# The first feed-forward's first pass: inner tiles that take 5 to 14 channel tiles, and another mix and pace behind it

## The chip, the core and the metric

The kernel runs on one core of one Trainium2 chip. TensorE (PE) multiplies, VectorE (DVE) and ScalarE (ACT) do the elementwise work, SyncE (SP) issues every DMA, GpSimd (POOL) does next to nothing. The metric is the time of one execution in device microseconds. Three runs of the kernel before gave a median of 1883.54 us (1883.38 to 1883.9).

## The reference, cut to what matters

One layer on 256 tokens of 2048 channels, in float32. The vector `c` gives nine modulation vectors of 2048 numbers each, by one matrix of 2048 x 18432.

```python
mod = silu(c) @ w_ada + b_ada                    # 2048 -> 9 x 2048
sh1, sc1, gt1, sh2, sc2, gt2, sh3, sc3, gt3 = split(mod, 9)
f = swiglu(modulate(rms_norm(h, g_ffn1), sh1, sc1), w1_gate, w1_up, w1_down)
h = h + 0.5 * gt1 * f
nrm = modulate(rms_norm(h, g_mix), sh2, sc2)
q, k, v = split(nrm @ w_qkv, 3)                  # then two kinds of attention
h = h + gt2 * mix
f = swiglu(modulate(rms_norm(h, g_ffn2), sh3, sc3), w2_gate, w2_up, w2_down)
h = h + 0.5 * gt3 * f
# swiglu(x) = (silu(x @ w_gate) * (x @ w_up)) @ w_down, inner width 5632
```

## The kernel before, in words

Channels lie in 16 tiles of 128 (`KT`), the inner width in 44 tiles (`FT`). All weights come in one stream (`W`, in the order of `srcs`) of chunks of 512 KB; a chunk is eight blocks of 128 x 128. A chunk in `rw` is split: ACT casts it to the short format (`hiw`, `wsplit`), DVE subtracts that from the original (`low`), and four buffers hold each (`LOB`). SP fetches three chunks ahead (`AHEAD`). The activations `nx[k]` are split in the same way.

A block costs PE a fixed amount. In the wide form (`mm2`) it is one matmul of 512 columns and one of 256; in the slim form (`mm3`) three of 256. The very first blocks are not split: there PE multiplies in float32 ("native", the loop over `K1` in `build`, line 561).

The modulation vectors are made beside it. One step takes a row block of `w_ada` (1 MB, `ada_issue`), and DVE reduces it against `cb` into one column of one vector (`ada_use`, tiles `ra` and `rx`, line 151). A channel tile `k` of `nx` needs two of them, the scale and the shift. Steps wait in the list `bg`. `bg_step` issues the DMA of the next step and, when all three buffers are taken, first reduces an older one; `pend` holds what is issued and not reduced yet. How many steps are made is set by `ws.pace(rate)`: each chunk fetched adds `rate` to a credit, and each whole credit makes one step. `bg_until(n)` makes steps until only `n` are left, and its reductions stand in the program where it is called.

The first feed-forward then runs in these passes.

- Native: inner tiles 0 to 7 take the first `K1` channel tiles while the modulation comes in.
- First part (`up_first`, tiles `pa`, weights `w1_a`): inner tiles 8 to 31 take the first `K1` channel tiles, too, at pace `RA`; even ones slim, odd ones wide. Each partial sum is parked in SBUF (`park`, `park2`, tiles `pt`).
- Later pass (`ffn`, tiles `pb`, weights `w1_b`): inner tiles 0 to 3 take the other channel tiles by the steps of `CUTS`, as they come; then 4 to 31 take theirs, each added to what was parked and passed through the gate on DVE and ACT (`up_finish`). The pace is `RB[0]`.
- Down (`ffn_down`, tiles `pd`, weights `w1_d`) at `RB[1]`; the twelve inner tiles left over, up (`pb`, `w1_c`) at `RB[2]` and down (`pd`, `w1_e`) at `RB[3]`. The last four are slim on the last output tile, `d` = 15.

From the last cut on, the list `bg` holds the 64 steps of the modulation vectors 2, 4, 3 and 5 (gate of this feed-forward; scale, shift and gate of the attention). After the last down pass `build` calls `bg_until(0)`, issues some idle matmuls (`idle(14)`, tile `pw`), and computes from the sum of squares (`stat`, `rstd_first`) the first `nx` of the attention, whose q, k and v matmuls (`pqv`, `pqk`, `pqq`) follow.

The order on each engine is a strict queue, made when the program is built: the framework sorts the instructions by program order, priority and its own estimate of when they are ready. PE alone keeps the order written in the attention.

Of the kernel before, what the change touches and what calls it, by code (L numbers as in the profile page):

```python
# [15 lines left out]
P = 128  # L16
S = 256
D = 2048
KT = D // P
DFF = 5632  # L20
FT = DFF // P
# [2 lines left out]
EPS = 1e-6  # L24
NEG = -1e30
CW = 1024
K1 = 6
K2 = 8
CUTS = (6, 8, 10, 12, 14, 16)
CUTS2 = (8, 12, 16)  # L30
NF0 = 8
NF1 = 4
NL = 4
ND = 3
F1 = 32
PLAN = ((4, 6, 9, 11), (8, 10, 13, 15), (12, 14, 17, 19), (16, 18, 21, 23))
PLAN_L = ((4, 6, 9, 11), (6, 8, 11, 13), (7, 9, 12, 14), (9, 11, 14, 15))
QS = 1
PACT = 0
RA = 0.455  # L40
RB = (0.28, 0.36, 0.36, 0.3)
RQ = 0.2
RE = 0.28
RF = (0.2, 0.2, 0.1, 0.1)
# [8 lines left out]
PLACE = ((44, 40),) + 7 * ((48, 0),)  # L53
KA = 3
SLIM = 4
MANUAL = {mybir.EngineType.PE}


# [10 lines left out]
def build(tc, a):  # L69
    nc = tc.nc  # L70
    with ExitStack() as ctx:
# [202 lines left out]
        def bg_add(ids, then=None):  # L274

            ids = list(ids)
            bg.extend((i, then if i == ids[-1] else None) for i in ids)
# [115 lines left out]
        ws = W()  # L393

        def up_first(f, part, kx, slim=False):
            ps = pair("pa")
            if slim:
                for j in range(2):
                    for k in range(kx):
                        wh, wl = ws.next()  # L400
                        mm3(ps[:, j, :S], wh, wl, nx[k][:, 0, :], nx[k][:, 1, :], k == 0, k == kx - 1)
                park(ps[:, :, :S], f, part)
                return
            up_mm(ps, 0, kx, True, True)
            park2(ps, f, part)
# [20 lines left out]
        def up_mm(ps, k0, k1, first, last):  # L426
            for j in range(2):
                for k in range(k0, k1):
                    mm2(ps[:, j, :], *ws.next(), nx[k], first and k == k0, last and k == k1 - 1)
# [17 lines left out]
        def ffn_down(fs, hid, gate, stat=None, out=None):  # L447
            acc_ = {}
            for d, f in down_order(fs):
                if d not in acc_:  # L450
                    acc_[d] = bank("pd")
                slim = d == KT - 1 and (stat is not None or out is not None)
                if slim:
                    wh, wl = ws.next()
                    mm3(acc_[d][:, :S], wh, wl, hid[f][:, 0, :], hid[f][:, 1, :], f == fs[0], f == fs[-1])
                else:
                    mm2(acc_[d], *ws.next(), hid[f], f == fs[0], f == fs[-1])
                if f != fs[-1]:
                    continue
                ps = acc_[d]  # L460
                g = gate(d)
                if d == KT - 1 and stat is not None:
                    idle(3)
                with tc.high_priority(offset=URGENT if stat is not None and d >= KT - 2 else 0):
                    for part_ in (ps[:, :S],) if slim else (ps[:, :S], ps[:, S:]):
                        nc.vector.scalar_tensor_tensor(h[d], part_, g, h[d], ALU.mult, ALU.add)  # L466
                    if stat is not None:
                        stat.add(h[d])
                        if d == KT - 1:
                            ws.split_late(stat.sq)  # L470
                if out is not None:
                    nc.sync.dma_start(out[d], h[d])

        def ffn(cuts, part, ready_k, gate, rates, stat=None, out=None):

            kx = cuts[0]
            hid = {}
            head = [pair("pb") for f in range(NF1)]
            for k0, k1 in zip(cuts, cuts[1:]):
                ready_k(k1)  # L480
                if k1 == KT:
                    late[:] = [True]
                    ws.pace(rates[0])
                for f in range(NF1):
                    up_mm(head[f], k0, k1, k0 == kx, k1 == KT)
                    if k1 == KT:
                        up_finish(f, head[f], part, hid)
            for f in range(NF1, F1):
                ps = pair("pb")
                up_mm(ps, kx, KT, True, True)  # L490
                up_finish(f, ps, part, hid)
            psum_pool("bank")
            ws.pace(rates[1])
            ffn_down(range(F1), hid, gate)
            psum_pool("pair")
            ws.pace(rates[2])
            for f in range(F1, FT):
                ps = pair("pb")
                up_mm(ps, 0, KT, True, True)
                up_finish(f, ps, {}, hid)  # L500
            ln_exp_set()
            psum_pool("bank")
            ws.pace(rates[3])
            ffn_down(range(F1, FT), hid, gate, stat, out)

# [4 lines left out]
        part = {}  # L510
# [41 lines left out]
        for k in range(K1):  # L552
# [4 lines left out]
            for j in range(2):  # L557
                w = ws.whole()
                for b in range(8):
                    f, q = 4 * j + b // 2, b % 2  # L560
# [8 lines left out]
                after(ins, casts[f // 3 - 1], "cast")  # L569
        psum_pool("pair")  # L570

        ws.pace(RA)
        for f in range(NF0, F1):
            up_first(f, part, K1, f % 2 == 0)
        st = Stat(KT)

        def rest1(k):
            bg_until(min(len(bg) + len(pend), (KT - k) * 2))
            if k < KT:
                return  # L580
            for j in (2, 4, 3, 5):
                bg_add(j * KT + k for k in range(KT))

        def once(l, fn):
            def get(d):
                if (l, d) not in gates:
                    gates[l, d] = fn(d)
                return gates[l, d]
            return get
# [4 lines left out]
            bg_until(min(len(bg) + len(pend), 4 * KT - d - 1))  # L594
            return mods[2][:, d : d + 1]

        ffn(CUTS, part, rest1, once(1, gate1), RB, stat=st)
        ws.pace(0.0)
        bg_until(0)
        idle(14)  # L600
# [289 lines left out]
            bg_until(min(len(bg) + len(pend), KT - d - 1))  # L890
            return mods[8][:, d : d + 1]

        ffn(CUTS2, part, rest2, once(3, gate3), RF, out=a["out"])
        psum_pool(None)
        ax_close()

# [1 line left out]
def _consts():  # L898
# [22 lines left out]

_SHAPES = {
    "x": (4, P, 4, S), "w_ada": (9 * KT, P, D), "vecs": (P, 224),
    "w1_s": (K1 * 2, P, CW), "w1_a": ((F1 - NF0) * 2 * K1 // 8, P, CW),
    "w1_b": (F1 * 2 * (KT - K1) // 8, P, CW), "w1_c": ((FT - F1) * 2 * KT // 8, P, CW),
    "w1_d": (KT * F1 // 8, P, CW), "w1_e": (KT * (FT - F1) // 8, P, CW),
    "w2_a": (F1 * 2 * K2 // 8, P, CW),
    "w2_b": (F1 * 2 * (KT - K2) // 8, P, CW), "w2_c": ((FT - F1) * 2 * KT // 8, P, CW),
# [6 lines left out]
def _arrays(inputs):  # L935
    g = {k: np.asarray(v) for k, v in inputs.items()}
    rope, lnc, nam, idx = _consts()
    c = np.ascontiguousarray

    def vec(v):  # L940
        return np.asarray(v).reshape(-1, P).T

    arr = {
        "x": c(g["x"][0].T.reshape(4, 4, P, S).transpose(0, 2, 1, 3)),
        "w_ada": c(g["w_ada"][0].reshape(D, 9 * KT, P).transpose(1, 2, 0)),
        "vecs": c(np.concatenate([
            vec(g["g_ffn1"][0]), vec(g["g_mix"][0]), vec(g["g_ffn2"][0]),
            vec(g["g_out_na"][0]), vec(g["g_out_dil"][0]), vec(g["c"][0]), vec(g["b_ada"][0])], axis=1)),
        "qkg": c(np.stack([g["qn_na"][0], g["kn_na"][0], g["qn_dil"][0], g["kn_dil"][0]])),
        "rope": rope, "lnc": lnc, "nam": nam,  # L950
        "nab": c(g["rpb_na"][0].reshape(8, -1)[:, idx].reshape(8, 2, P, S).transpose(0, 2, 1, 3)),
        "w_qkv": c(g["w_qkv"][0].reshape(8, 2, P, 3, 4, 512).transpose(4, 3, 0, 2, 1, 5)[:, ::-1].reshape(96, P, CW)),
        "w_o": c(g["w_o"][0].reshape(2, 8, P, KT, P).transpose(0, 3, 2, 1, 4).reshape(2 * KT, P, CW)),
    }

    def stream(blocks):
        return c(blocks.reshape(-1, 8, P, P).transpose(0, 2, 1, 3).reshape(-1, P, CW))

    for l in (1, 2):
        gu = np.stack([g[f"w{l}_gate"][0], g[f"w{l}_up"][0]]).reshape(2, KT, P, FT, P)  # L960
        gu = gu.transpose(3, 0, 1, 2, 4)
        cuts = CUTS if l == 1 else CUTS2
        kx = cuts[0]
        down = g[f"w{l}_down"][0].reshape(FT, P, KT, P).transpose(2, 0, 1, 3)

        def flat(x):
            return x.reshape(-1, P, P)

        if l == 1:
            arr["w1_a"] = stream(gu[NF0:F1, :, :kx])  # L970
        else:
            arr["w2_a"] = stream(np.concatenate([
                flat(gu[:NF1, :, :KA].transpose(2, 0, 1, 3, 4)), flat(gu[:NF1, :, KA:kx]),
                flat(gu[NF1:F1, :, :kx])]))
        arr[f"w{l}_b"] = stream(np.concatenate([
            *(flat(gu[:NF1, :, k0:k1]) for k0, k1 in zip(cuts, cuts[1:])), flat(gu[NF1:F1, :, kx:])]))
        arr[f"w{l}_c"] = stream(gu[F1:])
        for nm, fs in (("d", range(F1)), ("e", range(F1, FT))):
            d, f = np.array(list(down_order(fs))).T
            arr[f"w{l}_{nm}"] = stream(down[d, f])  # L980
        if l == 1:
            arr["w1_s"] = stream(gu[:NF0, :, :K1].transpose(2, 0, 1, 3, 4))
    return arr
# [21 lines left out]
```

## Time and profile before

| | |
|---|---|
| median of three runs | 1883.54 us |
| profiled execution, its time | 1883.25 us |
| its span | 1881.4 us |
| PE, DVE, ACT busy | 99%, 82%, 48% of the span |
| native pass, 96 blocks | 18.04 to 63.03 us |
| first part, 288 blocks (36 chunks) | 63.03 to 166.18 us |
| later pass, 640 blocks (80 chunks) | 166.18 to 384.37 us |
| rest of the first feed-forward | 384.37 to 755.35 us |
| first q, k, v matmul | 760.17 us |

A matmul's duration in the profile runs to the modelled end of its pipeline, so consecutive ones overlap, and what a block costs is read from the start of one to the start of the next. DVE instructions overlap their neighbours by some 70 to 80 ns as well. "PEclk" is the granted share of the TensorE clock. The stretches in the table begin and end where PE's output tile changes its name.

### The profile page before, as it was taken

The numbers are of one execution on the slowest core, as the hardware profiler recorded it, in microseconds if no ns is written. First come the engines' busy times: TensorE is split into PE (matmuls) and PEld (weight loads), VectorE is DVE, ScalarE is ACT, GpSimd is POOL, SyncE is SP. The second block draws the span as 40 slices with busy tenths as digits, with TensorE's granted clock in tenths as the row PEclk, the third lists the DMA queues.
The fourth block names the chain that finished last, engine by engine and source line by source line (L and its number), as shares of the span: only waits on it lengthen the run. The fifth ranks groups of instructions, "written<-read, shape, count | busy, mean of one in ns | idle before, by whom it ended". The sixth has DMA issues, their size and how long they took to land.

```text
span 1881.4 us, 27865 instructions
## 1 busy us (share of the span) xinstructions
PE 1867.2 (99%) x10744; PEld 1639.4 (87%) x10744; DVE 1549.2 (82%) x2105; ACT 905.9 (48%) x1331; POOL 0.7 (0%) x6
## 2 busy tenths in 40 slices
PE   8999999999999999999999999999999999999999
PEld 6998888888888888888888889888888888888888
DVE  7898999988888889878887899888799975556665
ACT  2454554443334454545555565544555543334442
POOL 0000000000000000000000000000000000000000
PEclk9999999999999999999999999999999999999999
DMA  9998887889899987777766456888677876666664
GB/s 394 391 354 314 306 306 292 313 330 333 327 336 322 334 307 252 260 259 247 259 224 201 148 167 214 301 303 289 221 267 270 281 269 212 193 192 194 195 204 136
DMA packets 120229, 504.02 MB, mean 268 GB/s; under 512 B 13344, under 2 KB 15904, under 8 KB 101664
## 3 DMA queue, kind: packets, MB, share of 16 engines
q1 hardware_dynamic: 120096, 502.24, 76.6%
q8 instruction: 84, 1.38, 0.3%
q14 instruction: 49, 0.40, 0.1%
HBM read 500.09 MB, written 2.10 MB: 267 GB/s over the span
## 4 chain that ended last, share of the span: by engine, by line
PE 96%; DVE 2%; DMA 2%; ACT 0%; issue 0%; ACTq 0%; DVEq 0%
PE pb L177 23%; PE pd L177 17%; PE pb L178 12%; PE pd L178 8%; PE pa L177 8%; PE pqv L183 5%; PE pqk L183 5%; PE pqq L183 5%; PE pa L178 4%; PE pso L177 3%; PE pa L183 2%; DMA rx<-in_w_ada_dram 2%; PE pso L178 1%; DVE rx L151 1%; PE pso L183 1%; PE psc L183 1%
## 5 line engine op out<-in xcount | busy, mean ns | idle before, releaser
L171 ACT CAST hiw<-rw 128x1024 fp32r<-128x1024 f32 x644 | 674.2, 1050 | 716.8 <-PE pd L177 230.4
L172 DVE TENSOR_TENSOR low<-rw,hiw 128x1024 fp32r<-128x1024 f32 x644 | 784.6, 1221 | 253.3 <-ACT hiw L171 252.1
L177 PE MATMUL pb<-nx,hiw 128*128 128x512 f32 x1920 | 654.5, 389 | 0.0
L178 PE MATMUL pb<-nx,low 128*128 128x256 f32 x1920 | 530.3, 276 | 0.0
L177 PE MATMUL pd<-hd,hiw 128*128 128x512 f32 x1384 | 471.9, 389 | 0.0
L177 PEld LDWEIGHTS pb<-nx,hiw 128*128 128x128 f32 x1920 | 360.3, 188 | 75.6
L178 PE MATMUL pd<-hd,low 128*128 128x256 f32 x1384 | 382.5, 276 | 0.0
L178 PEld LDWEIGHTS pb<-nx,low 128*128 128x128 f32 x1920 | 360.4, 188 | 0.2
L177 PEld LDWEIGHTS pd<-hd,hiw 128*128 128x128 f32 x1384 | 259.8, 188 | 54.6
L178 PEld LDWEIGHTS pd<-hd,low 128*128 128x128 f32 x1384 | 259.8, 188 | 0.0
L151 DVE CUSTOM_DVE_ANT_0 ra<-ra,cb,vec 128x2048 f32<-128x2048 f32 x101 | 236.9, 2346 | 3.3 <-DMA ra<-in_w_ada_dram 3.3
L177 PE MATMUL pa<-nx,hiw 128*128 128x512 f32 x656 | 224.7, 390 | 0.6 <-DVE nx L268 0.6
L178 PE MATMUL pa<-nx,low 128*128 128x256 f32 x656 | 181.6, 277 | 1.3 <-DVE low L172 1.3
L177 PEld LDWEIGHTS pa<-nx,hiw 128*128 128x128 f32 x656 | 123.2, 188 | 25.9 <-PE pw L194 0.8
L178 PEld LDWEIGHTS pa<-nx,low 128*128 128x128 f32 x656 | 123.1, 188 | 1.9 <-DVE low L172 1.9
L151 DVE CUSTOM_DVE_ANT_0 rx<-rx,cb,vec 128x2048 f32<-128x2048 f32 x43 | 100.9, 2345 | 1.8 <-DMA rx<-in_w_ada_dram 1.8
L183 PE MATMUL pqk<-hiw,nx 128*128 128x512 f32 x256 | 84.4, 395 | 0.0
L183 PE MATMUL pqq<-hiw,nx 128*128 128x512 f32 x256 | 83.0, 393 | 0.0
L183 PE MATMUL pqv<-hiw,nx 128*128 128x512 f32 x256 | 81.6, 393 | 0.0
L177 PE MATMUL pso<-ox,hiw 128*128 128x512 f32 x224 | 78.8, 396 | 0.0
L466 DVE SCALAR_TENSOR_TENSOR h<-pd,m,h 128x256 f32<-128x256 f32 x126 | 59.8, 481 | 20.9 <-PE pd L178 14.8
L178 PE MATMUL pso<-ox,low 128*128 128x256 f32 x224 | 62.6, 279 | 0.7 <-DVE low L172 0.7
(159 smaller groups left out, 1704.2 us busy)
## 6 DMA issues: line engine op xcount, KB each, us to landing
ra<-in_w_ada_dram SPq DMA_DIRECT2D x101, 1024.0 KB, 7.2
rw<-in_w_b_dram SPq DMA_DIRECT2D x144, 512.0 KB, 4.7
rw<-in_w_d_dram SPq DMA_DIRECT2D x128, 512.0 KB, 4.4
rw<-in_w_a_dram SPq DMA_DIRECT2D x100, 512.0 KB, 5.1
rw<-in_w_c_dram SPq DMA_DIRECT2D x96, 512.0 KB, 4.4
rw<-in_w_qkv_dram SPq DMA_DIRECT2D x96, 512.0 KB, 4.3
rx<-in_w_ada_dram SPq DMA_DIRECT2D x43, 1024.0 KB, 7.3
rw<-in_w_e_dram SPq DMA_DIRECT2D x48, 512.0 KB, 4.5
```

The source lines that it names most:

```text
L151: ins = nc.vector.tensor_tensor_reduce(out=raw, in0=raw, in1=cb, scale=1.0, scalar=vec[:, BA + i : BA + i + 1], op0=ALU.mult, op1=ALU.add, ...
L171: casts[:] = casts[-1:] + [nc.scalar.copy(hi, raw)]
L172: lows[:] = lows[-1:] + [nc.vector.tensor_tensor(lo, raw, hi.bitcast(F32), ALU.subtract)]
L177: nc.tensor.matmul(out, lh, r, start=first, stop=False)
L178: nc.tensor.matmul(out[:, :S], ll, r[:, 0, :], start=False, stop=last)
L183: nc.tensor.matmul(out, l, r, start=first and i == 0, stop=last and i == 2, **kw)
L466: nc.vector.scalar_tensor_tensor(h[d], part_, g, h[d], ALU.mult, ALU.add)
```

## The change

The native pass takes five channel tiles instead of six. In the first part each inner tile has its own number of channel tiles, given by `SEEN`: 5 for inner tiles 0 to 11, then rising to 14 for 30 and 31. `rest1(SEEN[f])` sees to it that the program has made the steps which tile `f` needs. Only tiles with at most 6 are slim: 8 to 14. The first part so has 416 blocks (52 chunks), the later pass 528 (66 chunks). There the order is `MIX`: 0 to 3, then 4, 31, 5, 30 and so on, a tile with many channel tiles left and one with few. The cuts are 5, 13, 15 and 16, and the paces `RA` and `RB` change. The host lays the weight stream out to match. The second feed-forward gets constants that leave it as it was.

```diff
-K1 = 6
+K1 = 5
-CUTS = (6, 8, 10, 12, 14, 16)
+CUTS = (K1, 13, 15, 16)
+SEEN = 8 * (K1,) + (5, 5, 5, 5, 6, 6, 6, 7, 7, 7, 8, 8, 8, 9, 9, 10, 10, 11, 11, 12, 12, 13, 14, 14)
+MIX = tuple(range(NF1)) + tuple(f for i in range(14) for f in (NF1 + i, F1 - 1 - i))
-RA = 0.455
-RB = (0.28, 0.36, 0.36, 0.3)
+RA = 0.42
+RB = (0.17, 0.4, 0.4, 0.3)
...
-            for f in range(NF1, F1):
+            for f in fs[NF1:]:
                 ps = pair("pb")
-                up_mm(ps, kx, KT, True, True)
+                up_mm(ps, seen[f], KT, True, True)
                 up_finish(f, ps, part, hid)
...
         ws.pace(RA)
         for f in range(NF0, F1):
-            up_first(f, part, K1, f % 2 == 0)
+            rest1(SEEN[f])
+            up_first(f, part, SEEN[f], SEEN[f] <= 6)
...
-        ffn(CUTS, part, rest1, once(1, gate1), RB, stat=st)
+        ffn(CUTS, SEEN, MIX, part, rest1, once(1, gate1), RB, stat=st)
```

Two places of the new order matter below. (The changed file has three or four lines more, so that its line 154 is line 151 of before, and so on.)

The first is DVE's queue at the end of the first feed-forward, from the last output tile (`h`, d = 15) to the first steps of the next norm. `ISA ra` or `rx` is a reduction of a modulation step (with the short row under it that reads its sum out), `sq` the last square of the statistics, `rs`, `nt` and `rsr` belong to the norm. Before:

```order
L466 SCALAR_TENSOR_TENSOR h_82<-pd,m_90,h_82 128x256 x2
L251 TENSOR_TENSOR sqa<-sqa,sq 128x256
L466 SCALAR_TENSOR_TENSOR h_82<-pd,m_90,h_82 128x256
L241 TENSOR_TENSOR sq<-h_82 128x256
L172 TENSOR_TENSOR low<-rw,hiw 128x1024
L222 TENSOR_SCALAR rs_7164<-pstat 128x256
L225 SCALAR_TENSOR_TENSOR nt<-h_79,m_92,rsr 128x256
L226 TENSOR_TENSOR rs_7163<-rs_7163,rs_7164 128x256
L227 SCALAR_TENSOR_TENSOR nt<-rs_7163,nt 128x256
```

And now:

```order
L469 SCALAR_TENSOR_TENSOR h_82<-pd,m_90,h_82 128x256
L154 ISA ra_7097,m_93<-ra_7097,cb,vec 128x2048
L154 ISA m_93 128x1
L244 TENSOR_TENSOR sq<-h_82 128x256
L175 TENSOR_TENSOR low<-rw,hiw 128x1024
L154 ISA rx_7100,m_93<-rx_7100,cb,vec 128x2048
L154 ISA m_93 128x1
L225 TENSOR_SCALAR rs_7123<-pstat 128x256
L228 SCALAR_TENSOR_TENSOR nt<-h_79,m_92,rsr 128x256
L229 TENSOR_TENSOR rs_7122<-rs_7122,rs_7123 128x256
L154 ISA ra_7103,m_93<-ra_7103,cb,vec 128x2048
L154 ISA m_93 128x1
```

Three reductions have come in between the last output tile and the norm; the row after the last one shown is the counterpart of line 227. Two more (`rx_7053`, `ra_7094`) stand just ahead of these rows, around the output tile d = 14 and the last `low` of the feed-forward.

The second is SP's queue at the end of the native pass: `rw` are weight chunks (`w_s` native, `w_a` the first part), `ra` and `rx` the steps, of which `rx_338` and `ra_347` before and `rx_342` and `ra_351` now belong to channel tile 5. Before:

```order
L142 DMA ra_305<-in_w_ada_dram 128x2048
L142 DMA ra_314<-in_w_ada_dram 128x2048
L163 DMA rw<-in_w_s_dram 128x1024 x2
L142 DMA rx_338<-in_w_ada_dram 128x2048
L142 DMA ra_347<-in_w_ada_dram 128x2048
L163 DMA rw<-in_w_s_dram 128x1024 x2
L163 DMA rw<-in_w_a_dram 128x1024 x2
```

And now:

```order
L145 DMA ra_305<-in_w_ada_dram 128x2048
L145 DMA ra_314<-in_w_ada_dram 128x2048
L166 DMA rw<-in_w_s_dram 128x1024 x2
L166 DMA rw<-in_w_a_dram 128x1024 x2
L145 DMA rx_342<-in_w_ada_dram 128x2048
L145 DMA ra_351<-in_w_ada_dram 128x2048
L166 DMA rw<-in_w_a_dram 128x1024 x3
```

The last two native chunks are gone, and the first two chunks of the first part have moved ahead of the steps of channel tile 5.

More of the change, by code (lines that the diff above doesn't have):

```diff
@@ L55 @@
 SLIM = 4
+SEEN2 = F1 * (K2,)
 MANUAL = {mybir.EngineType.PE}
@@ L472, in ffn_down, with ffn @@
                     nc.sync.dma_start(out[d], h[d])
-        def ffn(cuts, part, ready_k, gate, rates, stat=None, out=None):
+        def ffn(cuts, seen, fs, part, ready_k, gate, rates, stat=None, out=None):
             kx = cuts[0]
@@ L484, in ffn @@
                 for f in range(NF1):
-                    up_mm(head[f], k0, k1, k0 == kx, k1 == KT)
+                    up_mm(head[f], k0, k1, k0 == seen[f], k1 == KT)
                     if k1 == KT:
                         up_finish(f, head[f], part, hid)
-            for f in range(NF1, F1):
+            for f in fs[NF1:]:
                 ps = pair("pb")
-                up_mm(ps, kx, KT, True, True)
+                up_mm(ps, seen[f], KT, True, True)
                 up_finish(f, ps, part, hid)
@@ L493, in ffn @@
             ws.pace(rates[1])
-            ffn_down(range(F1), hid, gate)
+            ffn_down(fs, hid, gate)
             psum_pool("pair")
@@ L570, in build @@
         psum_pool("pair")
-        ws.pace(RA)
-        for f in range(NF0, F1):
-            up_first(f, part, K1, f % 2 == 0)
-        st = Stat(KT)
         def rest1(k):
@@ L582, in rest1 @@
                 bg_add(j * KT + k for k in range(KT))
+        ws.pace(RA)
+        for f in range(NF0, F1):
+            rest1(SEEN[f])
+            up_first(f, part, SEEN[f], SEEN[f] <= 6)
+        st = Stat(KT)
         def once(l, fn):
@@ L891, in gate3 @@
             return mods[8][:, d : d + 1]
-        ffn(CUTS2, part, rest2, once(3, gate3), RF, out=a["out"])
+        ffn(CUTS2, SEEN2, range(F1), part, rest2, once(3, gate3), RF, out=a["out"])
         psum_pool(None)
@@ L923 @@
     "x": (4, P, 4, S), "w_ada": (9 * KT, P, D), "vecs": (P, 224),
-    "w1_s": (K1 * 2, P, CW), "w1_a": ((F1 - NF0) * 2 * K1 // 8, P, CW),
-    "w1_b": (F1 * 2 * (KT - K1) // 8, P, CW), "w1_c": ((FT - F1) * 2 * KT // 8, P, CW),
+    "w1_s": (K1 * 2, P, CW), "w1_a": (sum(SEEN[NF0:]) * 2 // 8, P, CW),
+    "w1_b": ((F1 * KT - sum(SEEN)) * 2 // 8, P, CW), "w1_c": ((FT - F1) * 2 * KT // 8, P, CW),
     "w1_d": (KT * F1 // 8, P, CW), "w1_e": (KT * (FT - F1) // 8, P, CW),
@@ L961, in _arrays @@
         gu = gu.transpose(3, 0, 1, 2, 4)
-        cuts = CUTS if l == 1 else CUTS2
+        cuts, seen, order = (CUTS, SEEN, MIX) if l == 1 else (CUTS2, SEEN2, range(F1))
         kx = cuts[0]
@@ L969, in _arrays @@
         if l == 1:
-            arr["w1_a"] = stream(gu[NF0:F1, :, :kx])
+            arr["w1_a"] = stream(np.concatenate([flat(gu[f, :, : SEEN[f]]) for f in range(NF0, F1)]))
         else:
@@ L975, in _arrays @@
         arr[f"w{l}_b"] = stream(np.concatenate([
-            *(flat(gu[:NF1, :, k0:k1]) for k0, k1 in zip(cuts, cuts[1:])), flat(gu[NF1:F1, :, kx:])]))
+            *(flat(gu[:NF1, :, k0:k1]) for k0, k1 in zip(cuts, cuts[1:])), *(flat(gu[f, :, seen[f] :]) for f in order[NF1:])]))
         arr[f"w{l}_c"] = stream(gu[F1:])
-        for nm, fs in (("d", range(F1)), ("e", range(F1, FT))):
+        for nm, fs in (("d", order), ("e", range(F1, FT))):
             d, f = np.array(list(down_order(fs))).T
```

## The prediction

> **What bounds the kernel now.** I read the page first (busy shares, then the instruction groups), then the stretches of the first feed-forward with their busy times, then the timelines where PE waits.
>
> ```profile
> span 1881.4 us, 27865 instructions
> PE 1867.2 (99%) x10744; PEld 1639.4 (87%) x10744; DVE 1549.2 (82%) x2105; ACT 905.9 (48%) x1331; POOL 0.7 (0%) x6
> PE 96%; DVE 2%; DMA 2%; ACT 0%; issue 0%; ACTq 0%; DVEq 0%
> L172 DVE TENSOR_TENSOR low<-rw,hiw 128x1024 fp32r<-128x1024 f32 x644 | 784.6, 1221 | 253.3 <-ACT hiw L171 252.1
> ...
> L151 DVE CUSTOM_DVE_ANT_0 ra<-ra,cb,vec 128x2048 f32<-128x2048 f32 x101 | 236.9, 2346 | 3.3 <-DMA ra<-in_w_ada_dram 3.3
> ...
> ra<-in_w_ada_dram SPq DMA_DIRECT2D x101, 1024.0 KB, 7.2
> ```
>
> PE holds 96% of the chain. So the change can gain only where PE waits or does dearer work than it must, and it loses wherever it makes PE wait. The next view is the stretches: length, PE, weight loads, DVE, ACT, POOL (each with its count), clock, DMA share, GB/s. They are the native pass, first part, later pass, down, up, down; the last row is the later pass with the `pb` instructions alone.
>
> ```profile
> 18.04:63.03 44.99, 44.63 (x192) 38.20 (x193) 32.38 (x39) 10.38 (x20) 0.00 (x0) 0.94 1.02 415
> 63.03:166.18 103.15, 101.82 (x721) 94.82 (x721) 95.46 (x107) 51.81 (x68) 0.00 (x0) 1.00 0.96 361
> 166.18:384.37 218.19, 218.19 (x1283) 192.92 (x1281) 213.68 (x288) 109.63 (x146) 0.00 (x0) 1.00 0.83 301
> 384.37:558.88 174.51, 174.51 (x1027) 154.38 (x1026) 145.26 (x163) 68.16 (x67) 0.00 (x0) 1.00 0.91 334
> 558.88:689.75 130.87, 130.87 (x770) 115.74 (x769) 113.71 (x129) 63.08 (x81) 0.00 (x0) 1.00 0.90 324
> 689.75:755.35 65.60, 65.60 (x399) 58.45 (x398) 56.10 (x80) 32.56 (x43) 0.00 (x0) 1.00 0.76 260
> ...
> 166.18:384.37 218.19, 218.19 (x1280) 192.80 (x1280) 42.00 (x62) 0.00 (x0) 1.00 0.83 301
> ```
>
> A wide block is two matmuls: 218.19 / 640 = 0.341 us. The 512 of the down pass give the same (174.51 / 512), so from 166 us to 755 us PE never waits: nothing is to be had there. What is left is the native pass, the first part, and the way to the attention.
>
> **The native pass loses a sixth.** The timeline gives the two pieces of it.
>
> ```profile
> 18.04 37.64 PE L561 MATMUL pa<-xf,rw 128*128 128x256 f32 x160 [3.75 <-ACT xf L266]
> ...
> 56.03 7.17 PE L561 MATMUL pa<-xf,rw 128*128 128x256 f32 x32 [0.35 <-ACT xf L266]
> ```
>
> The five channel tiles that stay end at 55.7, less some 0.17 by which a matmul's record outlasts its place: 55.5. The pass now ends at 63.03, so 7.5 us go. Its 16 blocks come back wide: 16 x 0.341 = 5.5. Gain 2.0.
>
> Can the first part start that early? Its first two chunks now stand in SP's queue ahead of the steps of channel tile 5. The queue is DMA-bound (415 GB/s), so 1 MB put ahead delays these two steps by 1.05 MB / 415 GB/s = 2.5 us, and the first two `low` by nothing. On DVE the third `low` waits behind both reductions; it falls due after 16 slim blocks. I find it ready within half a microsecond of that, and take 0 (bounds 0 and 1.5, half a reduction and a `low`).
>
> **Slim tiles.** One slim tile half of before, 36 matmuls, stands in the chain:
>
> ```profile
> 139.63 4.25 PE pa L183 x36
> ```
>
> That is 12 blocks, 0.354 us each, 13 ns more than a wide one. There were 144 slim blocks, now 4 x 10 + 3 x 12 = 76. Gain 68 x 0.013 = 0.9.
>
> **Waits in the first part.** Its 103.15 us hold 144 x 0.354 + 144 x 0.341 = 100.1 of work, so PE waits 3.1 us, 1.25 of them in one place at 162 us, where a `low` stood behind a reduction:
>
> ```profile
> 159.27 2.35 DVE L151 CUSTOM_DVE_ANT_0 rx<-rx,cb,vec 128x2048 f32<-128x2048 f32 x1
> ...
> 162.26 2.36 DVE L172 TENSOR_TENSOR low<-rw,hiw 128x1024 fp32r<-128x1024 f32 x2
> ```
>
> Now the part is 76 x 0.354 + 340 x 0.341 = 142.8 us long, with 52 chunks and 52 x 0.42 = 22 steps. It must load 52 x 0.524 + 22 x 1.049 = 50.3 MB, 352 GB/s (361 before). DVE was 95.46 / 103.15 = 93% busy; 16 more `low` at 1.22, 5 more reductions at 2.35 and some 6 us of norm and parking give 133 / 142.8 = 93%. So the density is the same, and waits in proportion would be 4.3 us; none at all is the other bound. The one of 1.25 us arose at the end, where now ten `low` follow each other without a reduction, so I scale only the remaining 1.8: 2.5 us. Gain 0.6.
>
> Each tile also needs its channel tiles made in time. By the credit, step 2(k - 4) has been reduced before the tile that first uses channel tile k begins, with one to three chunks (some 2.8 us each) in hand, so I add no wait; a late one is a rival below.
>
> **The later pass.** It keeps all 32 finishes, and has 528 blocks: 180.0 us. DVE was at 213.68 of 218.19 with PE unhindered. From that go 14 `low` (17.1) and, at pace 0.17 instead of 0.28, some 14 reductions (33): about 162 of 180, 90%. Locally it is tighter, since four finishes come on one chunk (two before) and the short tiles follow; a wait of 0 to 2 us, and I take 0. DMA falls below 301 GB/s. The down and up passes go from pace 0.36 to 0.4: 0.04 x 1.05 MB more per 2.73 us, 15 GB/s on 334, under the 415 of the first row; DVE gains 0.04 x 2.35 us per chunk, from 83 to 87%. Cost 0.
>
> So the front gives 2.0 + 0.9 + 0.6 = 3.5 us; with no wait left 6.0, with all the bad ends about 0.
>
> **What the slower pace leaves over.** The 64 later steps and the two reductions still in flight need 66 credits. Before: 72 chunks x 0.28 = 20, 64 x 0.36 = 23, 48 x 0.36 = 17, 24 x 0.3 = 7; 67, enough. Now: 56 x 0.17 = 9, 64 x 0.4 = 25, 48 x 0.4 = 19, 24 x 0.3 = 7; 60. Four steps and six reductions are left for `bg_until(0)` at the end of the feed-forward, and in DVE's strict queue they stand around the last output tile. What stood there before:
>
> ```profile
> 750.92 1.23 DVE L172 TENSOR_TENSOR low<-rw,hiw 128x1024 fp32r<-128x1024 f32 x1 [1.16 <-ACT hiw L171]
> 752.07 1.00 DVE L466 SCALAR_TENSOR_TENSOR h<-pd,m,h 128x256 f32<-128x256 f32 x2
> ...
> 755.55 0.49 DVE L466 SCALAR_TENSOR_TENSOR h<-pd,m,h 128x256 f32<-128x256 f32 x1 [1.08 <-PE pd L183]
> 756.07 0.42 DVE L241 TENSOR_TENSOR sq<-h 128x256 f32<-128x256 f32 x1
> 756.41 1.22 DVE L172 TENSOR_TENSOR low<-rw,hiw 128x1024 fp32r<-128x1024 f32 x1
> 757.79 0.42 DVE L222 TENSOR_SCALAR rs<-pstat 128x256 f32<-128x256 f32 x1 [0.16 <-ACT rs L221]
> 758.24 0.48 DVE L225 SCALAR_TENSOR_TENSOR nt<-h,m,rsr 128x256 f32<-128x256 f32 x1
> 758.68 0.43 DVE L226 TENSOR_TENSOR rs<-rs,rs 128x256 f32<-128x256 f32 x1
> 759.14 0.42 DVE L227 SCALAR_TENSOR_TENSOR nt<-rs,nt 128x256 f32<-128x256 f32 x1
> ...
> 53.08 2.35 DVE L151 CUSTOM_DVE_ANT_0 ra<-ra,cb,vec 128x2048 f32<-128x2048 f32 x1
> 55.35 0.08 DVE L151 DVE_READ_ACCUMULATOR2_ANT m<- 128x1 f32 x1
> ```
>
> The last two rows give a reduction's place in the queue: 2.27 us. PE ends its last `pd` matmul at 755.35 and can begin with q, k and v only after the operation at 759.14 and an ACT pass, at 760.17. The three reductions now in between:
> - `ra_7097` between `h` and `sq`: 2.27, all of it in the chain, since the statistics wait for `sq`.
> - `rx_7100` between the `low` and L222: DVE would be free at 757.55. The ops at 757.79 and 758.24 have only to precede the one at 758.68, so 2.27 less 0.3 of idle time: 1.9.
> - `ra_7103` ahead of 759.14: 2.27.
> - `rx_7053` and `ra_7094` around d = 14: DVE has slack there (1.08 us before 755.55), but the last `low` now ends behind a reduction, about a microsecond after PE wants it. I take 0.7.
>
> Together 7.1 us. Their DMAs, 7.2 us from issue to landing, are issued a buffer's turn ahead; only `ra_7103` could land late. Bounds: 4.5 (two reductions whole), 9.1 (four).
>
> **PE's clock after the wait.** The stretches that follow are those at which the granted clock changes (6.83 us long), and two at the ends of feed-forwards.
>
> ```profile
> 10.05:16.86 6.81, 4.24 (x18) 3.04 (x16) 6.78 (x11) 2.51 (x6) 0.00 (x0) 1.00 1.01 417
> 16.88:23.69 6.81, 5.65 (x13) 4.54 (x14) 5.40 (x8) 0.91 (x2) 0.00 (x0) 0.50 1.01 415
> ...
> 754.16:760.98 6.82, 6.82 (x53) 6.18 (x51) 5.42 (x12) 2.34 (x6) 0.00 (x0) 1.00 0.60 193
> 1873.72:1880.54 6.82, 4.48 (x38) 4.28 (x36) 1.45 (x3) 0.00 (x0) 0.00 (x0) 1.00 0.11 38
> 1880.55:1881.40 0.85, 0.00 (x0) 0.00 (x0) 0.00 (x0) 0.00 (x0) 0.00 (x0) 0.50 0.00 0
> ```
>
> Two stretches in which PE worked 62% and 66% were followed by half clock. In the transition of before the idle matmuls cover it: 100%. Now these matmuls, some 3.7 us with the statistics, are issued once `sq` is done; PE then stands still for about 2 us ahead of them and 4 us behind them. A stretch there holds about 53% work, so I expect half clock for one stretch, of which PE works the last 4.4 us: 2.2 us lost, between 0 and 3.4 (a whole stretch).
>
> The Trainium skill, "TensorE: Matmul & The Clock Gate", Part 1, has the half clock return after one idle window of about 3.4 us, free-running. By that rule a pause of about 4 us holds a whole window only one time in six, and the loss would mostly be 0. The trace speaks against it as worded: the clock fell at 16.87, with 4.24 us of work in the stretch before.
>
> **The sum**, against the profiled execution (1883.25; 1881.4 of it span): -3.5 + 7.1 + 2.2 = +5.8, 1889.0. That execution lies 0.3 below the median of the runs, so 1889.3.
>
> **The rivals.**
> - The clock holds. For it: most work lies behind the waiting statistics, and the windows run free. Against it: the two rows at 0.50. -3.5 + 7.1 = 1887.1. This is also the skill's rule.
> - The front saves all: no PE wait left in the first part. For it: less DMA per us than before. Against it: DVE as dense as before. With the tail and the clock 1886.8.
> - Steps come late for the growing tiles. The first part hangs on one reduction per 6.5 us; a wait for one landing (7.2 us) at two or three tiles would cost some 5 us: 1894. Against it: one to three chunks in hand.
> - The other side: the reductions at the end fall into time that DVE has anyway, as far as one or none is in the chain. Then 1883.5 - 3.5 to -6.0 and up to 2.3 back: about 1879. It decides at a transition under 2.3 us longer. Against it: DVE's queue is strict, and the three rows stand between `h` and L227's counterpart.
>
> **How the numbers follow.** Forecast as worked out 0.52; clock holds 0.25; front saves all 0.08; late steps 0.10; the other side 0.05. The forecast's own spread is 1886.5 to 1892.5 (front 0.5 to 6, clock 2 to 3.4). From no more than 1 in 10 on either side comes the range, 1884.5 to 1893.5. What a measurement can tell from no change is 0.2%, 3.8 us: above 1887.3 is slower. Forecast 0.42 of its 0.52 there, late steps 0.10, clock holds 0.10, front 0.01: slower 0.63. Faster, below 1879.8, 0.05. The same 0.32.
>
> **What would show it.** Native pass end at about 55.5; first part 143 to 147 us long; later pass 180 us (0.341 per block), its end near 381; from the last `pd` matmul to the first `pqv` about 11 us instead of 4.8, with three reductions on DVE in between; a clock of 0.50 within some 6 us of that. The prediction is wrong if the transition stays under 7 us, or if the first part holds more than 6 us of PE waits.

## The result, and the profile after

The changed kernel takes 1892.14 us (median of five runs, 1891.0 to 1892.67) against 1883.54 for the kernel before in the same session. The ratio is 1.0045, with a 95% interval of 1.0033 to 1.0056: slower by 8.6 us. The prediction was 1889.3.

The profiled execution took 1891.68 us. The head of its page and the first row of the chain of waits:

```profile
span 1889.9 us, 27760 instructions
PE 1867.6 (99%) x10676; PEld 1636.8 (87%) x10676; DVE 1555.4 (82%) x2112; ACT 905.6 (48%) x1332; POOL 0.7 (0%) x6
PE 94%; DVE 3%; DMA 2%; ACT 0%; issue 0%; SPq 0%; ACTq 0%; DVEq 0%
```

PE is as busy as before in sum, but its share of the chain fell from 96 to 94%, and DVE's rose from 2 to 3%. The stretches of the first feed-forward tell where: native pass, first part, later pass, down, up, down (length, PE, weight loads, DVE, ACT, POOL, clock, DMA share, GB/s).

```profile
18.38:55.67 37.29, 37.11 (x160) 31.77 (x160) 26.62 (x32) 9.47 (x18) 0.00 (x0) 0.94 1.02 414
55.67:202.84 147.17, 144.85 (x910) 129.79 (x910) 132.87 (x146) 69.72 (x88) 0.00 (x0) 1.00 0.90 334
202.84:383.80 180.96, 180.43 (x1059) 159.33 (x1057) 165.15 (x238) 92.38 (x129) 0.00 (x0) 1.00 0.72 248
383.80:558.30 174.50, 174.50 (x1026) 154.29 (x1025) 149.20 (x168) 68.17 (x67) 0.00 (x0) 1.00 0.93 348
558.30:689.18 130.88, 130.88 (x770) 115.75 (x769) 116.80 (x132) 62.97 (x81) 0.00 (x0) 1.00 0.92 341
689.18:754.78 65.60, 65.60 (x399) 58.50 (x398) 62.46 (x86) 32.64 (x43) 0.00 (x0) 1.00 0.89 316
```

The front ends at 383.80, where it ended at 384.37 before: 0.6 us gained. The next three passes are as long as they were. Then comes the whole loss: from the last `pd` matmul to the first `pqv` it is 754.78 to 768.79, 14.01 us, before 4.82. From there on both kernels run alike; the last `pd` matmul of the second feed-forward ends 8.44 us later (1886.64 against 1878.20).

The chain of waits in that gap, in order of time (start, us, what):

```profile
744.35 11.37 DMA ra<-in_w_ada_dram
...
755.75 2.35 DVE ra L154
...
758.11 0.40 DVE h L469
758.51 2.26 DVE ra L154
...
760.77 0.34 DVE sq L244
761.11 1.13 DVE low L175
762.25 2.26 DVE rx L154
...
764.52 0.34 DVE rs L225
...
765.16 0.43 DVE rs L229
765.58 2.26 DVE ra L154
...
767.86 0.35 DVE nt L230
...
768.23 0.52 ACT nx L270
...
768.79 1.44 PE pqv L186 x4
```

Four reductions stand in the chain, one ahead of the last `h` and the three that the prediction named. From 755.75 to the pass of ACT at 768.23, DVE works through its queue almost without a pause.

In the front, PE waits for these (engine and line, who waited for whom, total, times, longest), from the first part to the end of the later pass:

```profile
PE pa L181 <- DVE low L175: 2.3, 4, 0.6
PE pb L180 <- DVE pt L441: 0.5, 1, 0.5
```

One of the four waits for a `low`, as the timeline of all engines shows it:

```profile
85.57 2.35 DVE L154 CUSTOM_DVE_ANT_0 ra<-ra,cb,vec 128x2048 f32<-128x2048 f32 x1
...
87.62 0.59 ACT L422 COPY pt<-pa 128x512 f32<-128x512 f32 x1 [3.23 <-PE pa L181]
...
88.10 1.05 ACT L174 CAST hiw<-rw 128x1024 fp32r<-128x1024 f32 x1
88.24 0.69 DVE L423 TENSOR_TENSOR pt<-pt,pa 128x512 f32<-128x512 f32 x1 [0.32 <-ACT pt L422]
...
89.19 1.23 DVE L175 TENSOR_TENSOR low<-rw,hiw 128x1024 fp32r<-128x1024 f32 x1 [0.26 <-ACT hiw L174]
...
89.46 0.39 PE L180 MATMUL pa<-nx,hiw 128*128 128x512 f32 x1
...
90.47 0.39 PE L181 MATMUL pa<-nx,low 128*128 128x256 f32 x1 [0.62 <-DVE low L175]
```

ACT stood idle for 3.23 us until PE had finished a wide tile, because the copy that parks it (L422) is ahead of the next chunk's cast (L174) in ACT's queue. Copy, cast and `low` then follow each other, and PE comes to that `low` too early. The matmul after the one at 89.46 should start 0.23 later and starts 1.01 later: 0.78 lost. (The waits listed above are smaller because a matmul's record outlasts its place.) The other three places lost 0.66 to 0.78 each.

### The profile page after: what moved, and what is told of

It reads as the page before. It is cut to its first block, busy times and chain, and to the rows that moved or that the text cites. A ratio compares the mean times of both kernels' runs of the same rounds, so it can differ in the third digit from the quotient of the medians.

```text
span 1889.9 us, 27760 instructions
## 1 busy us (share of the span) xinstructions
PE 1867.6 (99%) x10676; PEld 1636.8 (87%) x10676; DVE 1555.4 (82%) x2112; ACT 905.6 (48%) x1332; POOL 0.7 (0%) x6
## 4 chain that ended last, share of the span: by engine, by line
PE 94%; DVE 3%; DMA 2%; ACT 0%; issue 0%; SPq 0%; ACTq 0%; DVEq 0%
PE pb L180 22%; PE pd L180 16%; PE pb L181 11%; PE pa L180 10%; PE pd L181 8%; PE pa L181 5%; PE pqv L186 5%; PE pqk L186 5%; PE pqq L186 5%; PE pso L180 3%; PE pa L186 1%; PE pso L181 1%; DMA ra<-in_w_ada_dram 1%; DVE ra L154 1%; DVE low L175 1%; PE pso L186 1%
## 5 line engine op out<-in xcount | busy, mean ns | idle before, releaser
L174 ACT CAST hiw<-rw 128x1024 fp32r<-128x1024 f32 x646 | 675.7, 1050 | 708.8 <-PE pd L180 226.3
L180 PE MATMUL pb<-nx,hiw 128*128 128x512 f32 x1808 | 616.8, 389 | 0.5 <-DVE pt L441 0.5
L181 PE MATMUL pb<-nx,low 128*128 128x256 f32 x1808 | 499.8, 276 | 0.0
L180 PEld LDWEIGHTS pb<-nx,hiw 128*128 128x128 f32 x1808 | 339.4, 188 | 72.1 <-issue 0.8
L181 PEld LDWEIGHTS pb<-nx,low 128*128 128x128 f32 x1808 | 339.4, 188 | 0.0
L180 PE MATMUL pa<-nx,hiw 128*128 128x512 f32 x852 | 291.3, 390 | 0.6 <-DVE nx L271 0.6
L181 PE MATMUL pa<-nx,low 128*128 128x256 f32 x852 | 236.0, 277 | 2.3 <-DVE low L175 2.3
L180 PEld LDWEIGHTS pa<-nx,hiw 128*128 128x128 f32 x852 | 159.8, 188 | 34.2 <-PE pw L197 0.8
L181 PEld LDWEIGHTS pa<-nx,low 128*128 128x128 f32 x852 | 159.9, 188 | 4.1 <-DVE low L175 3.8
```

Source lines behind the costliest of these rows:

```text
L174: casts[:] = casts[-1:] + [nc.scalar.copy(hi, raw)]
L180: nc.tensor.matmul(out, lh, r, start=first, stop=False)
L181: nc.tensor.matmul(out[:, :S], ll, r[:, 0, :], start=False, stop=last)
```

## The experiments

All kernels were timed beside the kernel before, which had medians of 1883.25 to 1883.57 in these sessions.

| kernel | edit | median us | ratio to before (95%) | profiled us |
|---|---|---|---|---|
| t_before_short | kernel before, slow paces | 1892.11 | 1.0045 (1.0032 to 1.0059) | 1892.47 |
| t_done | changed, faster `pd` and up | 1887.25 | 1.0023 (1.0013 to 1.0032) | 1889.22 |
| t_three | changed, a little less of it | 1885.10 | 1.0010 (1.0001 to 1.0019) | 1886.75 |
| t_held | changed, left-overs moved | 1889.74 | 1.0032 (1.0020 to 1.0043) | 1887.48 |
| t_noidle | changed, no idle matmuls | 1893.36 | 1.0054 (1.0041 to 1.0068) | 1893.02 |
| t_spread | changed, more in the later pass | 1895.37 | 1.0063 (1.0051 to 1.0076) | 1893.26 |
| t_plain | t_spread, plain order | 1892.31 | 1.0051 (1.0039 to 1.0064) | 1892.29 |
| t_park | t_spread, copy behind cast | 1889.94 | 1.0039 (1.0027 to 1.0052) | 1893.19 |
| t_before_park | kernel before, copy behind cast | 1886.47 | 1.0017 (1.0008 to 1.0025) | 1884.69 |
| t_both | changed, both cures | 1878.86 | 0.9976 (0.9966 to 0.9986) | 1878.86 |
| t_both2 | the same, one step later | 1878.63 | 0.9976 (0.9966 to 0.9986) | 1878.24 |
| t_both_plain | t_both2, plain order | 1883.64 | 1.0001 (0.9992 to 1.0010) | 1883.32 |

The last column is the time of the one execution that the profile shows. In t_done, t_three and t_park it lies 1.7 to 3.3 us above the median, in t_held, t_spread and t_before_park 1.8 to 2.3 below; there the lengths of passes below stand for that execution, and need not add up to the median.

**The left-over steps alone: t_before_short.** The kernel before gets paces that leave as much over as the changed one has (60 credits for 66 steps).

```diff
-RB = (0.28, 0.36, 0.36, 0.3)
+RB = (0.13, 0.4, 0.4, 0.3)
```

> The kernel before with its paces changed from (0.28, 0.36, 0.36, 0.3) to (0.13, 0.4, 0.4, 0.3), which leaves four steps and six reductions for the end, as the changed kernel does; nothing else of the change. Theory 'tail': the end of the first feed-forward gets the same 14 us, 1883.5 + 9.2 = 1892.7 us. Rival 'front' (the loss comes with the new inner tiles): 1883.5 us.

The way to the attention took 13.79 us, and all passes ahead of it kept their times:

```profile
755.61:769.40 13.79, 8.25 (x40) 7.47 (x39) 13.75 (x19) 1.81 (x4) 0.00 (x0) 0.75 0.84 307
```

DVE worked 13.75 of the 13.79 us. So the pace alone, without any other part of the change, costs what the changed kernel lost there.

**All steps in time: t_done.** 9 + 30 + 22 + 7 = 68 credits.

```diff
-RB = (0.17, 0.4, 0.4, 0.3)
+RB = (0.17, 0.47, 0.46, 0.3)
```

> The changed kernel with the paces of the later pass and after it raised from (0.17, 0.4, 0.4, 0.3) to (0.17, 0.47, 0.46, 0.3), so that all 64 steps and their reductions are done before the last output tile. Theory 'tail' (the loss is the reductions left over on DVE at the end of the first feed-forward): the time from the last pd matmul to the first pqv falls from 14.0 to about 4.8 us, the kernel to 1892.1 - 9.2 = 1882.9 us. Rival 'front and pace' (the denser steps in the down passes, or the first part, cost it): it stays above 1888 us, and the down passes get longer.

The up pass and the way to the attention:

```profile
560.10:695.06 134.96, 133.04 (x770) 116.12 (x769) 124.15 (x137) 58.91 (x79) 0.00 (x0) 1.00 0.95 358
761.28:766.10 4.82, 4.82 (x41) 4.59 (x39) 4.32 (x9) 1.82 (x4) 0.00 (x0) 1.00 0.57 179
```

The gap is back at 4.82, but the up pass grew from 130.88 to 134.96 us. Twenty-two steps do not fit there beside the gates: PE waited there for a `low` of DVE, once for 1.5 us. (The first part, which this edit leaves as it was, took 148.64 us in that execution, 1.5 more than in the changed kernel's, so the median says more of the edit than this one time.) Each theory had half of it: the left-over steps are the loss, and where they are put matters.

**A little less: t_three.** `RB = (0.17, 0.44, 0.42, 0.3)`, 9 + 28 + 20 + 7 = 64 credits.

> The changed kernel with paces (0.17, 0.44, 0.42, 0.3): 63 credits of 66, so that one reduction is left in DVE's queue just ahead of the last output tile and none behind it. Theory 'tail': it costs what its landing and its 2.3 us reach beyond the last pd matmul, 0.5 to 3 us; 1883.4 to 1886 us. A rival in which the cost lies in the number of steps left and not in their place: half of 9.2, 1887.5 us.

One reduction stayed ahead of the last `h`, and the gap was 5.88 us (757.84 to 763.72). The up pass cost 0.6 more than in the changed kernel, the last down pass 1.05. The time is in the theory's range: what is left over costs by its place on DVE.

**The same left-overs, behind the norm: t_held.** The call `bg_until(0)` moves behind the sixteen norm tiles of the attention; nothing else changes.

```diff
         ws.pace(0.0)
-        bg_until(0)
         idle(14)
...
+        bg_until(0)
         ax_close()
```

> The changed kernel with bg_until(0) moved behind the 16 channel tiles of the next norm: as many steps are left over, but DVE reduces them after the norm. Theory 'tail' with the place on DVE deciding: transition about 4.8 us, 1883 us, perhaps 1 us more from the later reductions at the start of the attention. Rival 'the 4 MB on the DMA queues' (the left-over transfers delay the weights whatever DVE does): transition or the first q, k, v units longer by several us, 1886 us or more.

The gap is short again, and the loss turns up two passes later, in `pqk` (the first row is the gap, the second `pqk`, 21.76 us long before):

```profile
754.74:759.55 4.81, 4.81 (x40) 4.58 (x38) 4.32 (x9) 1.81 (x4) 0.00 (x0) 1.00 0.36 132
782.06:808.87 26.81, 22.97 (x98) 17.71 (x96) 26.81 (x28) 9.48 (x14) 0.00 (x0) 1.00 0.92 347
```

DVE was busy in all of `pqk`'s 26.81 us, and PE's longest wait for a `low` was 3.26 us. The median, 1889.74, is where the rival put it, but in the profiled execution PE waited for DVE there and not for a weight chunk. The reductions are not free in a place at which DVE is the one that PE waits for.

**Without the idle matmuls: t_noidle.** The line `idle(14)` behind `bg_until(0)` is dropped.

> The changed kernel without the idle matmuls (pw) between the first feed-forward and the attention. Theory (the half clock came, as the idle PE made it come, and fell on the idle matmuls, and they also gave it its end): now the half clock falls on the first q, k and v matmuls; the first pqv matmul starts where it did, 14.0 us behind the last pd, and the passes over q, k, v take 2 to 3.4 us more than their 22.53; 1894 to 1896. Rival (the clock comes back by itself after some 7 us, whatever PE does): no change, 1892.1, or up to 1 us less.

Two stretches of that kernel, both at half clock; the first `pqv` matmul starts at 767.92:

```profile
760.28:767.10 6.82, 1.22 (x2) 0.50 (x2) 6.82 (x9) 1.31 (x3) 0.00 (x0) 0.50 0.80 265
767.11:773.94 6.83, 6.02 (x14) 4.72 (x15) 6.72 (x15) 4.26 (x8) 0.00 (x0) 0.50 0.80 286
```

The half clock went on into q, k and v, whose first 96 matmuls took 24.72 us in place of 22.53: 2.2 lost. The gap itself came out 0.6 shorter (13.41). All of that lies ahead of the last `h`, which started 2.65 us behind PE's last `pd` instead of 3.24: in this execution the reduction in front of it did not have to wait for its step to land (0.33 of it), and DVE was less late. From that `h` to `pqv` it is 10.76 us against 10.77, so the idle matmuls do not lengthen the gap. The total rose by 1.2 to 1893.36 (across sessions), less than expected. The idle matmuls earn their place.

**More steps in the later pass: t_spread.** 15 + 28 + 17 + 7 = 67 credits, the up pass at the pace that it had before the change.

```diff
-RB = (0.17, 0.4, 0.4, 0.3)
+RB = (0.28, 0.44, 0.36, 0.3)
```

> Only the paces of the changed kernel differ: 0.28, 0.44, 0.36, 0.3 in place of 0.17, 0.4, 0.4, 0.3. 15 + 28 + 17 + 7 = 67 credits for 66 steps, so nothing is left over, and the up pass over the twelve inner tiles left keeps the pace that it had before the change (0.36). Theory (the loss is the left-over steps; the earlier cure lost in the up pass because that pass got denser): from the last pd matmul to the first q, k, v matmul 4.8 us, the up pass 130.9 and the last down pass 65.6 as before, the later pass 181 to 182.5; about 1883.0 (1882.3 to 1884.5), that is the kernel before less the 0.6 us that the front gained. Rival (some time is lost to the new order of steps wherever they lie): the steps that the later pass takes now make it wait there, 183 to 186 us, and the time stays at 1885 to 1888.

A miss, and for both theories. The gap (4.81), the up pass (130.88) and the last down pass (65.60) came out as expected, but the later pass and the first down pass did not:

```profile
202.30:389.35 187.05, 182.56 (x1058) 158.99 (x1057) 169.75 (x239) 92.16 (x128) 0.00 (x0) 1.00 0.79 270
389.35:569.04 179.69, 176.93 (x1026) 155.74 (x1025) 159.43 (x181) 68.50 (x68) 0.00 (x0) 0.99 0.93 352
```

6.1 and 5.2 us more than in the changed kernel. DVE's work in the two passes rose by 14.8 us (169.75 + 159.43 less 165.15 + 149.20), and PE paid 11.3 of it. DVE is busy for 91% of the later pass in both kernels; there was no room for six more steps (one more cost nothing in t_both, below). In the down pass two waits of 3.2 us in all, around 401 us, were followed by 3.4 us at half clock, 1.7 more.

**The plain order: t_plain.** Paces as in t_spread.

```diff
-MIX = tuple(range(NF1)) + tuple(f for i in range(14) for f in (NF1 + i, F1 - 1 - i))
+MIX = tuple(range(F1))
```

> As the kernel with paces 0.28, 0.44, 0.36, 0.3, but the later pass takes the inner tiles in the order 0 to 31 in place of the mixed one. Theory (in the later pass the work per inner tile is bound by DVE where a tile has few channel tiles left): inner tiles 28 to 31 have 4 to 2 channel tiles left and take DVE's nine instructions of the gate each, so that the end of the pass is bound by DVE: 3 to 8 us slower there than the mixed order. Rival (the gate's work has buffers enough to lag behind): within 1 us of the mixed order.

A miss: 1892.3, 3.1 us faster than the mixed order. The later pass took 183.89 and waited only at its end (1.5 and 1.6 us), the down pass 180.85. With too many steps in the pass the mixed order is the worse one; which of its waits the plain order avoids I did not separate.

**The copy behind the cast: t_park.** Paces as in t_spread.

```diff
         def park2(ps, f, part):
...
-            nc.scalar.copy(part[f], ps[:, :, :S])
+            after(nc.scalar.copy(part[f], ps[:, :, :S]), casts[-1], "cast")
```

> As the kernel with paces 0.28, 0.44, 0.36, 0.3, and in the first part ACT's copy of a finished wide tile (pt) is put behind the newest cast (hiw) on ACT's queue. Theory (the waits of 0.7 to 0.8 us in the first part come from the copy that stands ahead of the cast): the first part falls from 147.2 to 143 to 144 us, and the time is 3 us below that of the kernel with the same paces, about 1880. Rival (the waits come from DVE, which does a reduction of 2.3 us beside each second chunk): the first part stays at 146 to 148 us, since DVE is just as full, and PE waits for a low at other places.

The first part of t_park, and the same two places on ACT as in the timeline shown above:

```profile
55.88:198.84 142.96, 142.96 (x909) 129.46 (x909) 132.00 (x146) 71.21 (x88) 0.00 (x0) 1.00 0.92 349
...
83.55 2.00 ACT L174 CAST hiw<-rw 128x1024 fp32r<-128x1024 f32 x2
...
90.47 0.57 ACT L422 COPY pt<-pa 128x512 f32<-128x512 f32 x1
```

142.96 us without a wait, against 147.17 in the changed kernel and 146.90 in t_spread. DVE did the same 132 us of work in it, 92% busy. So the theory holds and the rival falls: not DVE's load but the order on ACT made these waits. The later pass then gave part of it back (189.43), as overfull as in t_spread.

**The same cure on the kernel before: t_before_park.**

> The kernel before, with ACT's copy of a wide tile behind the newest cast and nothing else changed. Theory (the 3.1 us of waits in its first part have the same cause as those of the changed kernel): first part 100.0 to 100.8 in place of 103.15, all else as it was, 1880.4 to 1881.2. Rival (before, these waits come from the reductions at pace 0.455): 102.5 to 103.2, 1883.0 to 1883.6.

The first part fell from 103.15 to 101.18, most of the way to the 100.0 to 100.8 of the theory, but the time rose. First part and later pass, and from DVE's timeline the reduction that stands ahead of the last gates:

```profile
63.11:164.29 101.18, 101.16 (x721) 94.46 (x721) 94.85 (x107) 52.45 (x69) 0.00 (x0) 1.00 0.96 366
164.29:385.71 221.42, 218.38 (x1282) 192.84 (x1281) 216.99 (x294) 110.20 (x148) 0.00 (x0) 1.00 0.83 302
...
380.22 2.34 DVE L151 CUSTOM_DVE_ANT_0 ra<-ra,cb,vec 128x2048 f32<-128x2048 f32 x1
```

The later pass, 218.19 before, is followed by one wait of 3.0 us, of the first down matmul for the last sums on DVE (`pt`, L438). DVE was 98% busy there, as it was before, so it seems that what came earlier in front had no place to go; no run tests this alone. The profile accounts for 1.3 of the 3.2 us by which the median rose; its execution was the fastest of that kernel.

**Both cures: t_both and t_both2.** The copy behind the cast, and 66 credits for 66 steps, placed where the passes had room: 10 + 30 + 19 + 7 in t_both, 9 + 30 + 19 + 8 in t_both2.

```diff
-RB = (0.17, 0.4, 0.4, 0.3)
+RB = (0.17, 0.47, 0.4, 0.34)
```

> The changed kernel with both cures: ACT's copy of a wide tile behind the newest cast, and paces 0.18, 0.47, 0.4, 0.3 (10 + 30 + 19 + 7 = 66 credits for 66 steps). Theory (the change gains some 6 us in front once the copies are out of the way of the casts, and loses it to five or six steps that find no place): first part 143, later pass 181 to 182, first pd pass 174.8, the rest as before, transition 4.8; about 1879.5 (1878.5 to 1881.5). Rival (the later pass is full at 0.17 already, so that one more step costs it 2 us, and the half clock follows a wait): 1882 to 1886.

> As the kernel with both cures, but the step that the later pass does not take is made in the last down pass: 0.17, 0.47, 0.4, 0.34 (9 + 30 + 19 + 8 = 66). Theory (each pass has room for a number of steps, and only what exceeds it costs): the later pass at 181.0, no wait; the last down pass at 65.6 to 66.3; 1879 to 1880.5. Rival (the last step comes too late, as its 1 MB lands over 11 us after its issue): the transition grows by 2 to 4 us and the time is 1881.5 to 1884.

1878.86 and 1878.63 us, the one step made no difference. First part, later pass, first down pass and the gap of t_both2:

```profile
55.51:198.47 142.96, 142.96 (x909) 129.45 (x909) 131.98 (x146) 71.22 (x88) 0.00 (x0) 1.00 0.93 350
198.47:379.19 180.72, 180.19 (x1059) 159.10 (x1057) 165.12 (x238) 92.39 (x129) 0.00 (x0) 1.00 0.70 244
379.19:553.96 174.77, 174.77 (x1026) 154.30 (x1025) 155.95 (x174) 68.21 (x67) 0.00 (x0) 1.00 0.96 369
...
750.51:755.33 4.82, 4.82 (x40) 4.59 (x38) 4.33 (x9) 1.82 (x4) 0.00 (x0) 1.00 0.59 160
```

This is the version that beats both: 4.6 us under the kernel before (medians of that session), 13.5 under the changed one (across sessions). The front now ends at 379.19, and nothing behind it is lost.

**What the mixed order is worth: t_both_plain.** t_both2 with `MIX = tuple(range(F1))`.

> As the kernel with both cures and paces 0.17, 0.47, 0.4, 0.34, but the later pass (and the down pass behind it) takes the inner tiles in the order 0 to 31 in place of the mixed one. Theory (short tiles one after the other ask more of DVE than their matmuls last): PE waits at the end of the later pass and at the start of the down pass, where the plain order at pace 0.28 waited 1.5, 1.6 and 4.2 us; with six steps (14 us of DVE) fewer in the pass some 1 to 4 us of that are left, 1879.6 to 1883. Rival (at a pace that DVE can hold the order does not matter): within 0.5 us of 1878.6.

```profile
198.76:381.00 182.24, 180.35 (x1059) 159.03 (x1057) 159.52 (x224) 91.88 (x126) 0.00 (x0) 1.00 0.72 246
381.00:559.01 178.01, 175.75 (x1025) 154.46 (x1025) 163.21 (x188) 68.82 (x71) 0.00 (x0) 1.00 0.93 357
```

5.0 us slower than t_both2 (across sessions): 1.5 in the later pass and 3.2 in the down pass, which starts while DVE still has gates of the short tiles to do (163.21 us of DVE work in the down pass against 155.95). At a pace that DVE can hold, mixing long and short tiles is what keeps PE going.

## Why the prediction was right or wrong

The sign and the main mechanism were right: the passes gain little, and steps left over at the end of the feed-forward cost more. By its steps:

- **Native pass.** Right: end at 55.67 (55.5 forecast). **Slim tiles.** Right: the first part without its waits is 142.96 us in t_park, 142.8 in the prediction.
- **Waits in the first part.** Mis-sized: 4.2 us (147.17 less 142.96), not 2.5. Scaling all waits of before gave 4.3, a bound that I named; I then left out the largest as a reduction's doing and scaled the rest by DVE's density. t_park shows that density was not the cause: with the same DVE work all waits go when ACT's copies leave the casts' way. Nor was the largest wait of before, 1.25 us, the reduction's doing alone: in t_before_park the same reduction (`rx`, from 157.41) stands ahead of the same `low`, and PE does not wait.
- **Later pass.** 180.96, not 180.0. Of this 0.69 us is one wait, where PE needs a buffer while the four heads are finished together on one chunk. The place was named, and 0 taken of 0 to 2. Together the front gave 0.6 us, not 3.5; it also began 0.3 later in this execution.
- **The paces 0.4.** Right: 174.50, 130.88 and 65.60, no cost.
- **The left-over reductions.** 9.2 us, not 7.1, just past the bound of 9.1 that stood for four whole ones. The three named rows came out near their 6.4, at 6.15 together. The term that failed is `rx_7053` and `ra_7094`, 0.7 in the prediction and 3.0 here. The last `h` began 0.20 us behind PE's last `pd` before, and 3.24 now (754.78 to 758.02). Of the 3.04, 2.27 is `ra_7094` itself, whole, ahead of `h`; 0.33 is DVE waiting until that step landed (755.42 to 755.75); 0.44 is what DVE was late already. The slack of 1.08 us that I counted on was used up by `rx_7053`. And the reason that I gave, a late last `low`, did not happen: the down pass kept its 65.60.
- **The clock.** It fell, as forecast, but wholly ahead of `pqv`, and cost nothing, not 2.2. These are four stretches of 3.4 us of the changed kernel, from where PE's matmuls ahead of the wait ended:

```profile
756.76:760.16 3.40, 0.00 (x0) 0.00 (x0) 3.40 (x4) 0.00 (x0) 0.00 (x0) 1.00 0.89 316
760.17:763.57 3.40, 2.40 (x9) 2.23 (x10) 3.40 (x5) 1.08 (x3) 0.00 (x0) 0.50 0.95 364
763.58:766.99 3.41, 3.41 (x18) 3.41 (x18) 3.41 (x6) 0.22 (x1) 0.00 (x0) 0.50 0.78 264
767.00:770.40 3.40, 2.40 (x13) 1.66 (x13) 3.29 (x9) 1.82 (x3) 0.00 (x0) 1.00 0.85 293
```

The half clock began at 760.2 and ended at 767.0, 1.8 us before the first `pqv`. It fell on the statistics and the idle matmuls alone. I had the idle matmuls done 4 us before `pqv`; at half speed and behind a longer wait (PE stood still for 4.4 us ahead of the statistics, not 2) they ran until about 767.8, and the full stretch that they made brought the clock back. t_noidle shows the other side: without them the forecast's 2.2 us are lost in q, k and v.

The sum: -0.6 + 9.2 + 0 = +8.6, where the prediction had -3.5 + 7.1 + 2.2 = +5.8. That the two lie within 2.8 us is in part luck: the gain of the front was put 2.9 us too high and the cost of the left-over reductions 2.1 too low, and the 2.2 for a clock that cost nothing made up for one of these. Of the rivals, "the clock holds" came nearest in its effect, though not in its mechanism. "The other side", about 1879, is what t_both2 gave once the steps fitted.

## What to carry to other kernels

When background work is metered by a pace, count what the paces yield and what is needed, and then ask of every pass how much the engine that does it can still take: here the paces were 6 short of 66, and two ways to make them up differ by 11 us (t_park and t_both2), and DVE's busy share of the later pass, about 90% in both, does not show it. A copy that waits for the bound engine must not stand ahead of the work that feeds that engine; an idle time on an engine that is 48% busy can be the cause of a stall that looks like another engine's. And a gain in one pass can be lost in the next, where that has no room for what now comes earlier.

## What the runs showed of the hardware that was not expected

**The granted clock moves in stretches of 3.41 us.** Every half-clock stretch looked at lasted a multiple of that: 3.41 in t_spread, 6.83 in the changed kernel, 13.65 in t_noidle. The clock came back behind the first 3.41 us that PE had used fully, or in t_plain to 90% (3.06 of 3.40 us from 402.66 on); 72% in the changed kernel (from 760.2 on) did not bring it back. It fell behind emptier ones: 0% in the changed kernel, and 45% in t_spread (the first row below, with the half clock in the second). In t_held 47% left the clock at 1.00 (the last row, within 0.1 us of a place of the same grid, counted from that run's earlier clock changes), but so did 42% in t_park (12.30 to 15.71 us). As the ends of matmuls are modelled, these traces give no sharp limit:

```profile
401.95:405.35 3.40, 1.53 (x9) 1.29 (x9) 3.40 (x5) 2.41 (x3) 0.00 (x0) 1.00 0.73 264
405.36:408.77 3.41, 3.41 (x13) 2.82 (x12) 3.41 (x5) 1.05 (x1) 0.00 (x0) 0.50 0.98 395
...
792.76:796.16 3.40, 1.60 (x8) 0.97 (x6) 3.40 (x4) 0.00 (x0) 0.00 (x0) 1.00 0.67 239
```

The Trainium skill, "TensorE: Matmul & The Clock Gate", Part 1, has a free-running activity window of about 3.4 us, an idle one of which halves the clock and a busy one restores it. These traces agree on the length and on the return; a window need not be wholly idle to halve the clock. The prediction read stretches of 6.83 us, two windows, and took 62% in them for enough to halve the clock, where each of its two rows held a full window and one of 24 or 31%.

**A step's landing can take half as long again.** A step of 1 MB took a median of 7.3 us from issue to landing in the changed kernel, and the one that the chain waited for 11.4 us. DMA moved 366 GB/s over these 11.4 us, against 267 over the whole execution; that the load is the reason is not shown.
